# Side work moved in a one-core encoder block: two sums of squares, the state space set-up, and two last scalings

## The chip, the cores and the metric

The kernel runs on one core of one Trainium2 chip. The metric is the device time of one execution in microseconds (us), as the median of three runs. The core has a matrix engine (TensorE, PE in the profile, with its weight loads as PEld), a vector engine (VectorE, DVE), an engine for functions of one operand (ScalarE, ACT), a general engine (GpSimd, POOL), and a queue that issues most DMAs (SyncE, SP). Each engine runs its own instructions strictly in order and waits on semaphores for the others.

## The reference

One layer of an encoder block on 1024 tokens of 1024 channels, in float32. Cut to what matters:

```python
h = h + 0.5 * swiglu(rms_norm(h, ffn1_norm), w_gate1, w_up1, w_down1)   # 1024 -> 2816 -> 1024
u = rms_norm(h, mix_norm);  z = u @ w_in
q, k, v, s_in, gates = split(z)
y_attn = neighbourhood_attention(q, k, v, rpb) @ w_attn_out
y_ssm  = s5_branch(s_in, lam, log_dt, b, c, d, glu) @ w_ssm_out         # state space layer, both directions
h = h + (g_attn * y_attn + g_ssm * y_ssm) @ w_out
h = h + 0.5 * swiglu(rms_norm(h, ffn2_norm), w_gate2, w_up2, w_down2)
h = h + (p @ w_ple) * sigmoid(rms_norm(h, ple_norm) @ w_ple_gate)
return rms_norm(h, final_norm)
```

`rms_norm(x, g)` is x * rsqrt(mean(x*x) + eps) * g over the channels.

## The kernel before

The activations are kept transposed, channels on the 128 partitions and tokens along the row, as eight channel tiles times two token halves `h[j][t]` of 128x512. A float32 product is made of three faster products: each operand is split into a rounded part and a rest (`split`, L152 to L154: a cast on ACT, a subtraction on DVE that writes `xl`, `wl` or `al`), and `mm3` (L181 to L186) multiplies high by high, high by low and low by high. One `mm3` is called a product here; it takes three PE instructions.

The two feed-forward layers use Strassen's scheme in its form with seven products (`Seven`, `Ffn`). A first tile of hidden units is computed plainly in four groups ("C" items: `11`, `12`, `22`, `21`, named after token half and column half). Layer 1 makes these groups with plain float32 matmuls (L651, two passes each), layer 2 with `mm3`. Then come ten pairs of hidden tiles p = 1 to 10 ("A" items, seven steps i, a gate `g` and an up branch `u` each, 14 items of 4 products per pair), and then the down projection ("B" items). The accumulators of an A pair are PSUM banks named x, y, z (`gx`, `ux`, ...). The bank `gx` is used by step 1, read out on DVE (L575), added to by step 3, used anew by step 5, read out again by L575, and added to by step 6. PE can't start step 3 or 6 before DVE has read the bank.

PE's order is the order in which the program is written. Side work is written as Python generators and driven by `tick()`, which is called after every product (in the plain groups after every L651 matmul): `yield n` means go on n products later. One generator chain runs beside layer 1:

- `early` (L351) norms the input: it waits 10 products, sums the squares of token half 0 over the channels with a matmul against a constant matrix (`stat`, `ms<-acc,ones`), takes the root (`rstd`: ACT's L205, then three DVE steps L206 to L208), scales the tiles (L349), and does the same later for half 1.
- `sums` makes the operands of the seven products.
- `gen_all` (L980) sets up the state space layer: `gen_params` is some 90 small DVE operations on 128x32 vectors (`pvec`, `pw`, `g_prm`); then for each of 16 pairs of state groups `gen_pair` builds matrices on POOL (`gm`, `em`, `bd`; L899 to L933), and `fin` turns them on PE 25 products later (40 for the last two): four transposes `tp` (L941) and four small matmuls `kp` (L952). After them 4 more products pass before the next pair.

Beside layer 2 runs `s7.second(10, 1)` (L364 on), which does for token half 1 what `early` does: after 10 products `ms<-acc,ones` (L251), the root, and the normed and split tiles for the groups `22` and `21`.

During the first part (up to the start of p = 2) the orders of PE, DVE and ACT are as written. From there to the last stage only PE's is; DVE's, ACT's, POOL's and SP's follow a planner that simulates the program and fills in what it finds ready, with some evacuations of PSUM ahead of the rest (`tc.high_priority`). Moving an item in the program therefore moves others too. The last stage, `end()` (L1676 on), is again in written order on DVE and ACT: the last two channel tiles (6 and 7) of the last 256 tokens are finished, the squares are summed, the root is taken, and `finish` multiplies (L1671) and stores pairs of tiles.

Of the kernel before, what the change touches and what calls it, by code (L numbers as in the profile page):

```python
# [25 lines left out]
NPAIR = 16  # L26
# [12 lines left out]
def encoder_block(ctx, tc, I, out):  # L39
# [38 lines left out]
    def thid(name, shape=(P, HT), dt=F32R):  # L78
        return at("hid", shape, dt, name)
# [4 lines left out]
    def tmq(name, shape=(P, HT)):  # L84
        return at("tmp", shape, F32, name)

    def bank(name):
        return ps.tile([P, HT], F32, tag="ps", name=name)
# [37 lines left out]
    def start(gen):  # L126
        side["gen"], side["wait"] = gen, next(gen, None)
        if side["wait"] is None:
            side["gen"] = None
# [71 lines left out]

        return tc.issue_after(mark["ins"]) if "ins" in mark else nullcontext()

    def rstd(m, r, q):
        A.activation(r, m, AF.Abs_reciprocal_sqrt, bias=eps)  # L205
        V.tensor_tensor(q, r, r, ALU.mult)  # L206
        V.scalar_tensor_tensor(q, m, eps, q, ALU.add, ALU.mult)
        V.scalar_tensor_tensor(r, q, -3.0, r, ALU.add, ALU.mult)  # L208

    class Norm:  # L210
# [30 lines left out]
            T.matmul(self.acc, lhsT=ones, rhs=sq, start=self.rest is None, stop=last)  # L241
            self.rest = sq

        def stat(self, r=None, summed=False):
            if summed:
                m = self.acc
            else:
                m = bank("ms")[:, 0:self.n]
                sums = [self.acc] + self.more
                for i, sq in enumerate(sums):  # L250
                    T.matmul(m, lhsT=ones, rhs=sq, start=i == 0, stop=i == len(sums) - 1)  # L251
            q = tmq("rq", [P, self.n])
            r = thid("rs", [P, self.n], F32) if r is None else r
            rstd(m, r, q)
            self.r = r

        def apply(self, gi, res, every):
# [35 lines left out]
    def after(n, fn):  # L293
        def gen():
            yield n
            fn()
        return gen()

    def chain(*gens):
        for g in gens:  # L300
            yield from g
# [8 lines left out]
    class Seven:  # L310
# [39 lines left out]

        def early(self):  # L351

            yield 10
            self.stat(0)
            for j in range(NK):
                self.gain(j, 1)
            yield 2
            for j in range(NK):
                self.scale(j, 0)
            yield 6  # L360
            for j in range(NK):
                self.add(j, 1)
            yield 2
            for k in range(4):  # L364
                self.put("a12", self.h[4 + k][0])
                yield 1
            yield 5
            self.stat(1)
            for k in range(4):
                self.put("a11", self.h[k][0])  # L370
            yield 6
            for j in (0, 4, 1, 5, 2, 6, 3, 7):
                self.scale(j, 1)
            yield 1
# [507 lines left out]
    def load_bc(pr):  # L882
        if pr < NPAIR:
            bcs[pr] = pools["g"].tile([P, 6, 2, 16], F32, tag="bc", bufs=1, name="bc")
            nc.sync.dma_start(bcs[pr], I["ssm_bc"][pr])
# [92 lines left out]
    s7 = Seven(h, 0, up)  # L978

    def gen_all():  # L980
        while "g" not in pools:
            yield 1
        yield from gen_params()
        load_bc(0)
        yield 10
        for pr in range(NPAIR):
            fin = gen_pair(pr)
            yield 25 if pr < NPAIR - 2 else 40
            fin()
            yield 4  # L990

# [8 lines left out]
    ffn = Ffn(s7, I["wg1"], I["wu1"], I["wd1"], a1_d, load_x, done, t0_done, (4, 7))  # L1000
# [581 lines left out]
    for n_, (i, j) in enumerate(steps):  # L1582
        if n_ == 4:
            s7 = Seven(h, 2)
            ffn = Ffn(s7, I["wg2"], I["wu2"], I["wd2"], a2_d, load_h2, done, t0_done2, (8, 11))
# [28 lines left out]
        ple_w(1)  # L1614

    ffn.hooks["B", 6, 2] = ple_ahead
    start(chain(s7.second(10, 1), ffn.sums(2)))
    ffn.run()
    drain()

# [15 lines left out]
    fin = [Fin(i) for i in range(3)]  # L1636

    def products(m, part):
        t, c0, c1 = parts[part] if part < 3 else (1, 0, HT)
        n = c1 - c0  # L1640
        a, b = bank("pg")[:, 0:n], bank("pp")[:, 0:n]
        for k in range(NK):
            mm3(a, W[m][k], [x[:, c0:c1] for x in pn[t][k]], k == 0, k == NK - 1)
            tick()
        for k in range(2):
            mm3(b, wpp[m // 4][(m % 4) * 2 + k], [x[:, c0:c1] for x in phl[k, t]], k == 0, k == 1)
            tick()
        return a, b, tmp("ps", [P, n]), h[m][t][:, c0:c1]
# [5 lines left out]
    def scaled(m, hm):  # L1654
        A.activation(hm, hm, AF.Copy, scale=gains[:, 4, m:m + 1])
# [22 lines left out]
    def end():  # L1678

        start(after(9, fin[1].stat))  # L1680
        six = products(6, 2)
        drain()
        finish(1, (0,))
        A.activation(six[2], six[0], AF.Sigmoid)
        added(*six)
        a, b, s, hm = products(7, 2)
        A.activation(s, a, AF.Sigmoid)
        fin[2].square(6, A)
        finish(1, (2,))

        A.activation(dummy, eps, AF.Abs_reciprocal_sqrt)
        scaled(6, six[3])
        added(a, b, s, hm)
        fin[2].square(7, V)
        scaled(7, hm)
        finish(1, (4, 6))
        fin[2].stat()
        finish(2)

    steps = [(m, 0) for m in range(4)] + [(m, 3) for m in range(4)] + [(m, 0) for m in range(4, NK)]  # L1700
# [109 lines left out]
```

## Time and profile before

| | us |
|---|---|
| median of 3 runs (lowest to highest) | 2099.49 (2098.23 to 2099.73) |
| the profiled execution, its own time | 2096.29 |
| its span, first to last instruction | 2094.5 |
| PE busy in the span | 2074.5 (99%) |
| DVE, ACT, POOL busy | 1416.1, 999.6, 399.4 |

The span is what the trace shows; 1.8 us of the profiled execution lie around it. The granted clock of TensorE was 0.998 of full speed over the whole span. PE is the engine to watch: what it does not compute, it waits, and every wait has a row with its releaser. Idle time of the others costs nothing by itself. A timeline row gives start, duration, engine, line, operation, shapes and, in brackets, how long the engine was idle before it and who ended that. Instructions of one engine overlap a little, so the next start can lie before the sum of start and duration.

### The profile page before, as it was taken

The numbers are of one execution on the slowest core, as the hardware profiler recorded it, in microseconds if no ns is written. First come the engines' busy times: TensorE is split into PE (matmuls) and PEld (weight loads), VectorE is DVE, ScalarE is ACT, GpSimd is POOL, SyncE is SP. The second block draws the span as 40 slices with busy tenths as digits, with TensorE's granted clock in tenths as the row PEclk, the third lists the DMA queues.
The fourth block names the chain that finished last, engine by engine and source line by source line (L and its number), as shares of the span: only waits on it lengthen the run. The fifth ranks groups of instructions, "written<-read, shape, count | busy, mean of one in ns | idle before, by whom it ended". The sixth has DMA issues, their size and how long they took to land.

```text
span 2094.5 us, 28063 instructions
## 1 busy us (share of the span) xinstructions
PE 2074.5 (99%) x9662; PEld 1705.4 (81%) x9662; DVE 1416.1 (68%) x2420; ACT 999.6 (48%) x1832; POOL 399.4 (19%) x636
## 2 busy tenths in 40 slices
PE   8999999999999999999999999999999999999998
PEld 3788888888888888888898888788888888888886
DVE  7897776667967334677753668995665665786855
ACT  6434333334445333667774635643333334445543
POOL 0037556441000006888200001000000000000000
PEclk9999999999999999999999999999999999999999
DMA  3435444475533551233477745243324238433302
GB/s 134 143 118 154 125 135 120 144 270 169 188 114 111 159 189 64 70 97 98 123 208 260 247 145 117 77 150 121 100 86 135 82 121 297 155 106 94 118 21 81
DMA packets 197744, 285.19 MB, mean 136 GB/s; under 512 B 41569, under 2 KB 81121, under 8 KB 197601
## 3 DMA queue, kind: packets, MB, share of 16 engines
q1 hardware_dynamic: 180304, 258.20, 38.8%
q10 hardware_dynamic: 14992, 21.00, 3.0%
q0 software_dynamic: 2304, 4.20, 1.2%
q8 instruction: 76, 1.25, 0.2%
q14 instruction: 68, 0.55, 0.1%
HBM read 201.01 MB, written 82.31 MB: 135 GB/s over the span
## 4 chain that ended last, share of the span: by engine, by line
PE 94%; DVE 2%; ACT 1%; DMA 1%; SPq 0%; issue 0%; DVEq 0%; ACTq 0%
PE dx L184 4%; PE dx L185 4%; PE dx L186 4%; PE gx L184 3%; PE ux L184 3%; PE ux L186 3%; PE gx L186 3%; PE gx L185 3%; PE ux L185 3%; PE gt L184 3%; PE gt L185 3%; PE gt L186 3%; PE dy L186 2%; PE dy L184 2%; PE dy L185 2%; PE gy L184 2%
## 5 line engine op out<-in xcount | busy, mean ns | idle before, releaser
L153 ACT CAST wh<-hbuf 128x512 fp32r<-128x512 f32 x280 | 173.0, 622 | 392.3 <-PE gx L185 80.9
L154 DVE TENSOR_TENSOR wl<-hbuf,wh 128x512 fp32r<-128x512 f32 x280 | 209.2, 750 | 122.7 <-ACT wh L153 120.5
L153 ACT CAST wh<-wblk 128x512 fp32r<-128x512 f32 x190 | 118.0, 622 | 192.6 <-PE dx L185 83.2
L154 DVE TENSOR_TENSOR wl<-wblk,wh 128x512 fp32r<-128x512 f32 x190 | 130.6, 690 | 49.3 <-ACT wh L153 41.8
L184 PE MATMUL dx<-ah,wh 128*128 128x512 f32 x416 | 163.3, 393 | 0.3 <-DVE hbuf L688 0.3
L186 PE MATMUL dx<-ah,wl 128*128 128x512 f32 x416 | 161.9, 389 | 0.0
L185 PE MATMUL dx<-al,wh 128*128 128x512 f32 x416 | 161.8, 389 | 0.0
L1092 POOL TENSOR_TENSOR sc<-X,rho 128x128 f32<-128x128 f32 x128 | 77.9, 609 | 327.2 <-ACT X L1075 317.3
L154 DVE TENSOR_TENSOR al<-araw,ah 128x512 fp32r<-128x512 f32 x154 | 106.3, 694 | 50.1 <-PE dx L185 21.1
L184 PE MATMUL gx<-xh,wh 128*128 128x512 f32 x320 | 124.9, 390 | 1.2 <-DVE c L575 1.2
L184 PE MATMUL ux<-xh,wh 128*128 128x512 f32 x320 | 125.0, 390 | 0.0
L186 PE MATMUL ux<-xh,wl 128*128 128x512 f32 x320 | 124.5, 389 | 0.0
L185 PE MATMUL gx<-xl,wh 128*128 128x512 f32 x320 | 124.5, 389 | 0.0
L186 PE MATMUL gx<-xh,wl 128*128 128x512 f32 x320 | 124.5, 389 | 0.0
L185 PE MATMUL ux<-xl,wh 128*128 128x512 f32 x320 | 124.5, 389 | 0.0
L153 ACT CAST ah<-araw 128x512 fp32r<-128x512 f32 x154 | 94.9, 619 | 43.2 <-PE dx L185 12.6
L184 PE MATMUL gt<-xh,wh 128*128 128x512 f32 x256 | 102.7, 401 | 0.0
L186 PE MATMUL gt<-xh,wl 128*128 128x512 f32 x256 | 99.8, 390 | 0.0
L185 PE MATMUL gt<-xl,wh 128*128 128x512 f32 x256 | 99.8, 390 | 0.0
L422 DVE TENSOR_TENSOR hbuf<-hbuf 128x512 f32<-128x512 f32 x120 | 91.4, 762 | 2.1
L184 PEld LDWEIGHTS dx<-ah,wh 128*128 128x128 f32 x416 | 78.1, 188 | 17.8 <-issue 0.7
L185 PEld LDWEIGHTS dx<-al,wh 128*128 128x128 f32 x416 | 78.1, 188 | 16.9 <-issue 0.7
(381 smaller groups left out, 5590.2 us busy)
## 6 DMA issues: line engine op xcount, KB each, us to landing
araw<-a_d SPq DMA_DIRECT2D x154, 256.0 KB
a_d<-c SPq DMA_DIRECT2D x148, 256.0 KB
wblk<-in_wd SPq DMA_DIRECT2D x88, 256.0 KB
hbuf<-in_wg SPq DMA_DIRECT2D x40, 512.0 KB
hbuf<-in_wu SPq DMA_DIRECT2D x40, 512.0 KB
wst<-in_win SPq DMA_DIRECT2D x26, 512.0 KB
hbuf<-in_xT SPq DMA_DIRECT2D x32, 256.0 KB
h_d<-hbuf ACTq DMA_DIRECT2D x32, 256.0 KB
```

The source lines that it names most:

```text
L153: A.copy(hi, src)
L154: return eng.tensor_tensor(lo, src, hi.bitcast(F32), ALU.subtract)
L184: T.matmul(o, lhsT=wh, rhs=xh, start=first, stop=False, skip_group_check=more)
L185: T.matmul(o, lhsT=wh, rhs=xl, start=False, stop=False, skip_group_check=more)
L186: T.matmul(o, lhsT=wl, rhs=xh, start=False, stop=last, skip_group_check=more)
L422: V.tensor_tensor(b11, (b12, b22, None, None, b21)[i - 2], b11, ALU.subtract)
L1092: G.tensor_tensor(sc, both, rho4, ALU.mult)
```

## The change

Three pieces of side work are written at other places; no arithmetic is added or taken away.

- Both sums of squares that a feed-forward layer takes beside its first products come two products later: `early` waits 12 instead of 10, and `second` 12 instead of 10.
- `gen_all` waits 56 products before `gen_params`, and the turned matrices stand 22 instead of 25 products behind their set-up. The transposes of the first pair come 53 products later in PE's order, those of each next pair 3 less, and from the fourteenth pair on 14.
- `rstd` gets a hook `mid` behind the root on ACT. In `end()` the two last scalings (L1655, tiles 6 and 7 times the gain) are given to it, so that ACT does them behind the last root instead of ahead of it.

```diff
-    def rstd(m, r, q):
+    def rstd(m, r, q, mid=None):
         A.activation(r, m, AF.Abs_reciprocal_sqrt, bias=eps)
+        if mid is not None:
+            mid()
         V.tensor_tensor(q, r, r, ALU.mult)
...
-        def stat(self, r=None, summed=False):
+        def stat(self, r=None, summed=False, mid=None):
...
-            rstd(m, r, q)
+            rstd(m, r, q, mid)
...
         def early(self):
 
-            yield 10
+            yield 12
             self.stat(0)
...
     def gen_all():
         while "g" not in pools:
             yield 1
+
+        yield 56
         yield from gen_params()
...
             fin = gen_pair(pr)
-            yield 25 if pr < NPAIR - 2 else 40
+            yield 22 if pr < NPAIR - 2 else 40
...
-    start(chain(s7.second(10, 1), ffn.sums(2)))
+    start(chain(s7.second(12, 1), ffn.sums(2)))
...
         A.activation(dummy, eps, AF.Abs_reciprocal_sqrt)
-        scaled(6, six[3])
         added(a, b, s, hm)
         fin[2].square(7, V)
-        scaled(7, hm)
         finish(1, (4, 6))
-        fin[2].stat()
+        fin[2].stat(mid=lambda: (scaled(6, six[3]), scaled(7, hm)))
         finish(2)
```

The line numbers of the changed kernel are 2 higher from L207 on and 4 higher from L987 on.

PE at the start of layer 1, before, in its own order (`g` and `u` are the gate and up banks of group `11`, one plain product each; in brackets what an instruction waits for):

```order
L651 MATMUL g_183<-xg,wblk 128x512 [waits DMAHW1_49,Activation_49]
L651 MATMUL u_184<-xg,wblk 128x512 [waits DMAHW2_49]
L345 MATMUL ms<-acc_112,ones 128x512 [waits DVE_49]
L651 MATMUL g_183<-xg,wblk 128x512 [waits Activation_49]
L651 MATMUL u_184<-xg,wblk 128x512
```

and now, from the same two products on:

```order
L653 MATMUL g_183<-xg,wblk 128x512 [waits DMAHW1_49,Activation_49]
L653 MATMUL u_184<-xg,wblk 128x512 [waits DMAHW2_49]
L653 MATMUL g_183<-xg,wblk 128x512 [waits Activation_49]
L653 MATMUL u_184<-xg,wblk 128x512
L347 MATMUL ms<-acc_112,ones 128x512 [waits DVE_49]
```

The sum of squares of half 0 stands behind the twelfth product instead of the tenth. The second one (`ms<-acc_113`) moves by two products as well, and the DVE operations that depend on them keep their order but for five that trade places with neighbours before 61 us.

DVE at steps 4 and 5 of p = 1, before (`g_prm` are the loaded state space parameters, `c` the hidden tiles, `wl` the rests of weights, `pvec` the set-up's vectors, `hbuf` the weight blocks that Strassen's scheme subtracts from each other):

```order
L422 TENSOR_TENSOR hbuf<-hbuf 128x512
L753 TENSOR_SCALAR g_prm<-g_prm 128x32
L780 TENSOR_SCALAR g_prm<-g_prm 128x32
L154 TENSOR_TENSOR wl<-hbuf,wh 128x512
L575 TENSOR_TENSOR c_621<-gy,c_621 128x512
```

and ten rows further:

```order
L581 TENSOR_TENSOR c_581<-c_600,c_581 128x512
L154 TENSOR_TENSOR wl<-hbuf,wh 128x512
L754 TENSOR_SCALAR pvec<-g_prm 128x32
L154 TENSOR_TENSOR wl<-hbuf,wh 128x512
L755 TENSOR_SCALAR pvec<-pvec 128x32
L422 TENSOR_TENSOR hbuf<-hbuf 128x512
```

Now, at the same two spots:

```order
L424 TENSOR_TENSOR hbuf<-hbuf 128x512
L755 TENSOR_SCALAR g_prm<-g_prm 128x32
L782 TENSOR_SCALAR g_prm<-g_prm 128x32
L154 TENSOR_TENSOR wl<-hbuf,wh 128x512
L577 TENSOR_TENSOR c_621<-gy,c_621 128x512
```

```order
L583 TENSOR_TENSOR c_581<-c_600,c_581 128x512
L154 TENSOR_TENSOR wl<-hbuf,wh 128x512 x2
L424 TENSOR_TENSOR hbuf<-hbuf 128x512
L426 TENSOR_TENSOR hbuf<-hbuf 128x512
L583 TENSOR_TENSOR c_738<-ux,c_738 128x512
```

The two clamps of `g_prm` stay where they were, and so does the load of `g_prm` in SP's order; the rest of the set-up, from the old L754 on, leaves this stretch and stands one pair p later.

PE in the group `11` of layer 2 (`u` is its up bank; one row is one of a product's three instructions, - before, + now):

```order
-L251 MATMUL ms<-acc,ones 128x512
+L184 MATMUL u_13097<-xh,wh 128x512
+L185 MATMUL u_13097<-xl,wh 128x512
+L186 MATMUL u_13097<-xh,wl 128x512
+L184 MATMUL u_13097<-xh,wh 128x512
+L185 MATMUL u_13097<-xl,wh 128x512
+L186 MATMUL u_13097<-xh,wl 128x512
+L253 MATMUL ms<-acc,ones 128x512
```

The sum of squares of half 1 stands two products later here too. On ACT the last root now stands ahead of the two scalings `hbuf<-hbuf,gains 128x256`, which stood ahead of it.

## Rows read from the trace of the kernel before

**Rows 1.** The page's first part: each engine's busy us, share of the span, instructions.

```profile
PE 2074.5 (99%) x9662; PEld 1705.4 (81%) x9662; DVE 1416.1 (68%) x2420; ACT 999.6 (48%) x1832; POOL 399.4 (19%) x636
```

**Rows 2.** Who PE waited for (first and last of eleven): us, times, longest.

```profile
PE g L651 <- ACT xg L336: 5.0, 1, 5.0
...
PE v L1393 <- DVE wl L154: 0.2, 1, 0.2
```

**Rows 3.** Timeline of PE at the start: both sums of squares among the products.

```profile
14.69 1.02 PE L651 MATMUL u<-xg,wblk 128*128 128x512 f32 x2
16.53 1.12 PE L345 MATMUL ms<-acc,ones 128*128 128x512 f32 x2 [0.82 <-DVE acc L341]
17.49 1.02 PE L651 MATMUL g<-xg,wblk 128*128 128x512 f32 x2
...
33.80 1.02 PE L345 MATMUL ms<-acc,ones 128*128 128x512 f32 x2
```

**Rows 4.** Timeline of ACT and DVE in the same stretch: roots, and what follows them.

```profile
17.70 0.69 ACT L205 ACTIVATE rs<-ms,eps 128x512 f32<-128x512 f32 x1 [0.64 <-PE ms L345]
...
35.58 0.69 DVE L206 TENSOR_TENSOR q<-rs 128x512 f32<-128x512 f32 x1 [0.32 <-ACT rs L205]
...
60.78 2.50 DVE L154 TENSOR_TENSOR wl<-hbuf,wh 128x512 fp32r<-128x512 f32 x4 [1.20 <-ACT wh L153]
```

**Rows 5.** Timeline of DVE and PE at steps 4 to 6 of p = 1.

```profile
92.58 0.18 DVE L753 TENSOR_SCALAR g_prm<-g_prm 128x32 f32<-128x32 f32 x1 [0.58 <-DMA g_prm<-in_ssm_p]
...
97.92 0.68 DVE L575 TENSOR_TENSOR c<-gx,c 128x512 f32<-128x512 f32 x1
...
98.76 0.47 PE L184 MATMUL gx<-xh,wh 128*128 128x512 f32 x1 [1.21 <-DVE c L575]
```

**Rows 6.** Timeline of DVE and POOL while POOL builds matrices, and PE's first transposes.

```profile
154.64 1.88 POOL L920 TENSOR_TENSOR em<-em,tg 128x576 f32<-128x576 f32 x1
...
148.82 1.65 DVE L536 TENSOR_TENSOR c<-c,c 128x512 f32<-128x512 f32 x1
...
157.71 0.68 DVE L575 TENSOR_TENSOR c<-gx,c 128x512 f32<-128x512 f32 x1
...
158.68 0.39 PE L184 MATMUL gx<-xh,wh 128*128 128x512 f32 x1
...
160.07 0.60 PE L941 MATMUL tp<-ident,gm 128*128 128x128 f32 x4
```

**Rows 7.** Timeline of DVE and PE at step 5 of p = 3, and DVE at a later pair of matrices.

```profile
174.18 0.69 DVE L575 TENSOR_TENSOR c<-gx,c 128x512 f32<-128x512 f32 x1 [0.76 <-PE gx L186]
...
176.70 0.39 PE L184 MATMUL gx<-xh,wh 128*128 128x512 f32 x1
...
226.49 1.66 DVE L422 TENSOR_TENSOR hbuf<-hbuf 128x512 f32<-128x512 f32 x1
228.07 1.92 DVE L532 TENSOR_TENSOR c<-c,c 128x512 f32<-128x512 f32 x1
```

**Rows 8.** Timeline of PE and DVE at the start of layer 2.

```profile
1341.07 1.12 PE L251 MATMUL ms<-acc,ones 128*128 128x512 f32 x2 [0.77 <-DVE acc L224]
...
1342.26 0.40 PE L185 MATMUL u<-xl,wh 128*128 128x512 f32 x1
...
1358.92 0.69 DVE L154 TENSOR_TENSOR xl<-hbuf,xh 128x512 fp32r<-128x512 f32 x1
...
1362.03 0.39 PE L185 MATMUL g<-xl,wh 128*128 128x512 f32 x1
```

**Rows 9.** Timeline of PE, ACT and DVE in the last stage.

```profile
2084.60 0.70 PE L251 MATMUL ms<-sq,ones 128*128 128x256 f32 x2 [0.70 <-DVE sq L232]
...
2084.57 0.89 ACT L1655 ACTIVATE hbuf<-hbuf,gains 128x256 f32<-128x256 f32 x2
2085.37 0.45 ACT L205 ACTIVATE rs<-ms,eps 128x256 f32<-128x256 f32 x1
...
2087.29 2.50 DVE L1671 TENSOR_TENSOR hbuf<-hbuf,rs 128x512 f32<-128x512 f32 x4
```

## The prediction

> **What bounds the kernel now.** First the page's first part: PE is busy for 2074.5 of 2094.5 us [rows 1], so the change can only give back what PE waits, and what PE computes is the same on both sides. So the next view is the list of PE's waits: eleven, the longest 5.0 us for the first operand, the shortest 0.2 us [rows 2]. Then the timelines around those that the change touches: 0.82 us ahead of the first sum of squares [rows 3], 1.21 us at step 6 of p = 1 [rows 5], 0.77 us ahead of the sum in layer 2 and 0.70 us ahead of the last one [rows 8, 9]. Between 100 and 640 us, where the set-up of the state space layer runs, PE waits nowhere. That sets the scale: all four waits together are 3.5 us, and about 0.2% of the time, 4.2 us, is what a measurement of this kernel can tell from no change.
>
> **The first sum of squares, two products later.** A plain product takes PE 0.858 us: 19 of them lie between 17.49 and 33.80 [rows 3]. Two are 1.72 us, and the wait that they fill is only 0.82. In the new order the sum starts three products behind the one at 14.69, at 17.26 instead of 16.53. It takes 1.02 us within a stream and took 1.12 after the stall [rows 3], so it ends at 18.28 instead of 17.65, and the root on ACT, which waited for nothing else [rows 4], starts 0.63 us later. PE itself is ahead: the next product but two started at 17.49 + 1.72 = 19.21 and now starts at 18.12, a gain of 1.09 us.
>
> Who waits for the root? DVE, and all behind it: from 18.4 us on DVE works through without a gap until it waits 0.32 us for the second root [rows 4]. That root comes from the second sum, which stands two products later on a PE that is 1.09 us ahead, so it is 1.72 - 1.09 = 0.63 late as well. Nothing in between gives the time back. The new DVE order brings the scaling of group `22` one split forward, which would free ACT's weight casts earlier, but in ACT's order that split's cast now stands behind it; DVE then waits its 1.20 us [rows 4] one row earlier, and the first weight rest starts where it did. From 60.78 to 98 us DVE and ACT wait for each other in turn and for the load of `g_prm` (0.58 us), not for PE. At 98.76 PE waits for the last of this chain, the read-out of bank `gx` that starts at 97.92 [rows 5].
>
> So I take it that the chain arrives 0.63 us later and PE with it: the 1.09 us gained are waited away there and **0.63 us are lost**. The bounds: -1.09 if the chain has slack that I don't see, +0.63 if it has none. I take the upper end, because the rows show DVE or ACT at work, or one waiting for the other, all the way.
>
> **The set-up, 56 products later.** The stall at 98.76 looks like the set-up's: DVE waited 0.58 us at 92.58 for `g_prm` [rows 5]. But the two clamps that wait for this load, and the load itself, keep their places in DVE's and SP's orders; only what is behind them moves, by 56 products of 0.68 us (29 lie between 1342.26 and 1362.03 [rows 8]), 38 us. So this wait stays, and the relief comes where PE had no wait to lose: zero.
>
> Moving it could cost something. PE's transposes come 53 products, 36.1 us, later in PE's order, so set-up and POOL have 3 products, 2.0 us, less. POOL finished the first `em` at 154.64 + 1.88 = 156.5, and PE began the transposes at 160.07 [rows 6]: 3.5 us of cover, and the set-up's last step now stands two items (5.4 us) earlier within its pair p. Later pairs follow each other every 26 products instead of 29; 26 x 0.68 + 1.7 for PE's own work is 19.4 us, and the first pair, set-up copies included, took POOL 15.5. SP and ACT get the same loads, stores and copies in other places; the weights that stand behind them on SP are two pairs p ahead. Cost zero, covered by these margins; the bound above is the second rival.
>
> While POOL builds a matrix, DVE slows: a `c<-c` took 1.65 us at 148.82 and a `c<-c,c` 1.92 at 228.07, against 0.69 otherwise, but a read-out of a PSUM bank stayed at 0.68 [rows 6, 7]. The Trainium skill says why (SBUF — State Buffer, Who interferes with whom): a VectorE instruction with two SBUF inputs contends with a GpSimd instruction that reads SBUF, for a lock and not for a share, and one with a single SBUF input doesn't. The trace agrees, with 1.65 and 0.68 us. By that rule the same POOL work costs DVE the same wherever it stands, which adds nothing to the sum as long as DVE's lag is covered.
>
> **The sum in layer 2, two products later.** Here the products are short. The last instruction ahead of the sum ended at 1341.07 - 0.77 = 1340.30; instructions take 0.39 us [rows 7] and start every 0.68 / 3 = 0.227, so it began at 1339.91. Six more follow, then the sum at 1341.50, the next product at 1342.36 and its second instruction at 1342.58. Before, that instruction stood at 1342.26 + 1.36 = 1343.62 [rows 8]: **1.04 us gained**. The sum ends at 1341.50 + 1.02 = 1342.52 instead of 1342.19, so the root is 0.33 us late. The tightest reader is the eighth product of group `22`: its operand's rest was done at 1358.92 + 0.69 = 1359.61, and PE read it at 1362.03 [rows 8]. Now it is done 0.33 later, and 0.60 more for one read-out that stands ahead of it, at 1360.54, and PE comes at 1360.99. Cover 0.45 us: no new wait. Bounds: -1.04, and 0 if the late root is paid back in group `22`.
>
> **The last scalings.** The two scalings took 0.89 us on ACT and the root started at 2085.37, right behind them [rows 9]. But it also needs the last sum. At the start a root began 17.70 - 16.53 = 1.17 us behind its sum [rows 3, 4]; this sum has half the columns and took 0.42 less (0.70 against 1.12), so it could let the root start at 2084.60 + 0.75 = 2085.35. I take 0.02 us gained; the bounds are 0 and 0.42 (one pass of the sum, 0.35 us, as its end). Behind the root the scalings are done by 2086.7, and the multiplication that reads them is the fourth of those from 2087.29 on, at 2089.1 [rows 9]: covered by 2.4 us.
>
> **The sum.** 2096.29 + 0.63 + 0 - 1.04 - 0.02 = 2095.86 for the profiled execution, 0.43 below it. That execution was 3.2 us faster than the median of the runs, so against the median I say 2099.49 - 0.43 = **2099.1**.
>
> **The rivals.**
>
> *The front keeps its gain.* If DVE's chain isn't the bound up to 98 us, or the planned order shortens it, the 1.09 us stay: -1.09 - 1.04 - 0.02 = -2.15, 2097.3. For it: PE's wait at 98.76 is for a single read-out. Against: DVE's gapless rows from 18 us on.
>
> *POOL's work falls on the tight read-out: slower.* Step 6 follows step 5 on the same bank, and DVE's read-out has 176.70 - 174.18 - 0.69 = 1.83 us to spare [rows 7]. A matrix build costs DVE about an extra 1 us for each of two or three operations (1.66 and 1.92 against 0.69 [rows 7]). By PE's orders, before, the builds began 10, 8 and 6 products ahead of the end of step 5's gate item at the nearest, and now two begin 7 and 3 ahead of it, one just behind it, and one just behind the up branch's item, four products later. If 3 us of lag meet 1.83 us of margin, each such pair costs some 1.2 us plus 0.2 for the restart. Up to four pairs lie so: +1.4 to +5.6, with the rest of the sum 2100.5 to 2104.7, and with two pairs 2101.9. It decides from 1.83 us of lag on. For it: the first build in the old order put DVE so far behind that a read-out which started at 157.71 left 0.3 us to the product at 158.68 [rows 6]. Against: in all later pairs PE never waited. By the Trainium skill's rule above this is where the contention would show.
>
> *The move takes the `g_prm` wait away after all.* If the load lands earlier, 0.58 + 0.18 us leave the chain: 2098.3.
>
> **How the numbers follow.** The forecast 0.60, the front keeping its gain 0.13, POOL's work on the read-out 0.21, `g_prm` 0.06. The range takes in the first rival, the second with two pairs, and the scatter of the runs (1.3 us below the median at the lowest): 2096.2 to 2102.3. Only the far end of the second rival is slower by over 4.2 us, and no case is faster by as much: faster 0.02, same 0.94, slower 0.04.
>
> **What would show it.** In the changed kernel's trace: no wait ahead of either moved sum; the first root at about 18.33; the wait at step 6 of p = 1 grown from 1.21 to more than 2 us and ending at about 99.4; DVE still waiting for `g_prm`; no PE wait at transposes; the next layer's sum without a wait; the last root at 2085.3 on the old clock. I am wrong if the wait at step 6 ends before 98.76, if PE waits between 100 and 500 us, or if the last root moves by over 0.4 us.

## The result, and the profile after

The changed kernel takes **2102.39 us** (median of 22 runs, 2099.17 to 2104.97), the kernel before, in runs on the same chips, 2098.69 (22 runs, 2096.22 to 2101.46). The ratio is 1.0017 [1.0011, 1.0024]: slower by 3.7 us, where the forecast was no change that can be told, 2099.1, with a range up to 2102.3.

The profiled execution of the changed kernel took 2104.40 us, its span 2102.6, against 2096.29 and 2094.5. The page's first part, as [rows 1]:

```profile
PE 2078.0 (99%) x9662; PEld 1707.6 (81%) x9662; DVE 1419.2 (67%) x2420; ACT 999.6 (48%) x1832; POOL 396.9 (19%) x636
```

PE has the same 9662 instructions and is busy 3.5 us more; the rest of the 8.1 us of span is waiting. PE's waits, which answer to [rows 2] (us in total, times, longest us):

```profile
PE g L653 <- ACT xg L338: 4.9, 1, 4.9
PE gx L184 <- DVE c L577: 4.5, 3, 2.0
PE yo L1121 <- DVE ot L1246: 2.0, 1, 2.0
PE ux L184 <- DVE c L577: 1.0, 2, 0.8
...
PE v L1397 <- DVE wl L154: 0.6, 1, 0.6
```

The waits for `acc` are gone from it, both in the front and in layer 2, as meant. But the list has waits on the read-outs of `gx` and `ux` (DVE's `c`, line 577) that before had one entry of 1.2 us. The timeline of PE, at the two moved sums and the last one and at the waits (start, us, operation, in brackets the idle time and who ended it):

```profile
17.13 1.02 PE L347 MATMUL ms<-acc,ones 128*128 128x512 f32 x2
...
83.49 0.47 PE L184 MATMUL ux<-xh,wh 128*128 128x512 f32 x1 [0.79 <-DVE c L577]
...
99.22 0.47 PE L184 MATMUL gx<-xh,wh 128*128 128x512 f32 x1 [1.85 <-DVE c L577]
...
302.83 0.50 PE L184 MATMUL ux<-xh,wh 128*128 128x512 f32 x1 [0.22 <-DVE c L577]
...
468.03 0.50 PE L184 MATMUL gx<-xh,wh 128*128 128x512 f32 x1 [1.96 <-DVE c L577]
...
1045.72 0.49 PE L1121 MATMUL yo<-emi 128*128 128x128 f32 x2 [2.02 <-DVE ot L1246]
...
1349.56 1.02 PE L253 MATMUL ms<-acc,ones 128*128 128x512 f32 x2
...
1403.04 0.50 PE L184 MATMUL gx<-xh,wh 128*128 128x512 f32 x1 [0.74 <-DVE c L577]
...
2092.69 0.70 PE L253 MATMUL ms<-sq,ones 128*128 128x256 f32 x2 [0.71 <-DVE sq L234]
```

To see what each wait is worth, the start of each product after is set against the same product before. How far PE is behind, profile against profile, worked out from the starts of the same instructions on both sides:

| place | PE behind, us | added here |
|---|---|---|
| start | 0.0 | |
| behind step 6 of p = 1 (100 us) | 0.5 | 0.5 |
| behind the wait at 303 us | 1.1 | 0.55 |
| last pair p, step 5 to 6 (468 us) | 4.9 | 3.9 |
| 767 us (`v<-wl`, a load) | 5.4 | 0.5 |
| 1046 us (`yo`) | 8.1 | 2.7 |
| layer 2, the sum | 7.0 | -1.07 |
| layer 2, step 6 of p = 1 | 8.1 | 1.05 |

The rows at 767 and 1046 us aren't the change's: the wait at 767 us is 0.65 us here and 0.21 in the second profile of the same kernel, and the one at 1046 us is shown below with the kernel before alone. Without the front (0.5 us) and the wait at 1046 us (2.7), 4.9 us are left, and 3.9 of them are one place at 468 us.

### The profile page after: what moved, and what is told of

Its sections match the earlier page's. It is cut to its first block, busy times and chain, and to the rows that moved or that the text cites. A ratio compares the mean times of both kernels' runs of the same rounds, so it can differ in the third digit from the quotient of the medians.

```text
span 2102.6 us, 28061 instructions
## 1 busy us (share of the span) xinstructions
PE 2078.0 (99%) x9662; PEld 1707.6 (81%) x9662; DVE 1419.2 (67%) x2420; ACT 999.6 (48%) x1832; POOL 396.9 (19%) x636
## 4 chain that ended last, share of the span: by engine, by line
PE 89%; DVE 7%; DMA 2%; ACT 1%; issue 1%; SPq 0%; DVEq 0%; ACTq 0%
PE dx L184 4%; PE dx L185 4%; PE dx L186 4%; PE gx L184 3%; PE ux L184 3%; PE gx L186 3%; PE gx L185 3%; PE ux L185 3%; PE ux L186 3%; PE gt L184 3%; PE gt L186 3%; PE gt L185 3%; PE dy L185 2%; PE dy L186 2%; PE dy L184 2%; PE gy L184 2%
## 5 line engine op out<-in xcount | busy, mean ns | idle before, releaser
L186 PE MATMUL dx<-ah,wl 128*128 128x512 f32 x416 | 161.9, 389 | 0.0
```

Of the source, the lines that this page charges most:

```text
L186: T.matmul(o, lhsT=wl, rhs=xh, start=False, stop=last, skip_group_check=more)
```

## The experiments

**Which part costs it.** Only the set-up's two numbers are put into the kernel before:

```diff
 # e1_setup_only: kernel before, with
+        yield 56
-            yield 25 if pr < NPAIR - 2 else 40
+            yield 22 if pr < NPAIR - 2 else 40
```

> Only the state space set-up is moved (56 products later, matrices 22 apart); sums of squares and last scalings stand as before. Theory A (the moved matrices run into the first loads of the down projection, SP holds those loads back, DVE waits for one of them ahead of the read-out of gx, PE stalls about 2 us near 468 us and then runs some 3 us at the lower clock): about 2102 us, with that wait in the trace, and the wait at step 6 of p = 1 at its old 1.2 us. Theory B (the late roots cost the time): no different from before, 2098.7 us, no wait of over 0.5 us between 100 and 700 us.

Measured 2101.64, ratio 1.0016 [1.0007, 1.0025]. Its profile has the wait near 468 us, at 1.24 us and without a lower clock behind it, and the old 1.20 us at step 6 of p = 1. The other way round, the changed kernel with the set-up put back:

```diff
 # e2_no_setup: kernel after, with
-        yield 56
-            yield 22 if pr < NPAIR - 2 else 40
+            yield 25 if pr < NPAIR - 2 else 40
```

> The two later sums and the scalings behind the last root, the set-up as before. Theory A: 2098.5 us, within 1 us of before (0.5 us lost at step 6 of p = 1, where the wait is about 1.8 us, and up to 1.0 us gained in layer 2), no wait between 100 and 700 us. Theory B: about 2102 us.

Measured 2098.75, 1.0001 [0.9992, 1.0010]. So the set-up has the loss, and the three other edits together come out at nothing that these runs can tell. Both kernels unchanged once more, for the scatter between two profiles of one kernel:

> The kernel before once more, for a second trace. If the waits near 468 and 1046 us of the changed kernel come from the change, this trace has none over 0.5 us between 100 and 700 us and 0.7 us at the attention's first wait (1039 us); if they are scatter of the transfers, one of them may show here too.

> The changed kernel once more, for a second trace. Theory A: the wait for the read-out of gx near 468 us is there again, 1.5 to 2.5 us, and 0.2 us or more at 303 us. Scatter: it is not. The wait of 2.0 us at 1046 us hangs on a store of y, and may be anything from 0.7 to 2.

They took 2099.25 and 2101.34, one run each. In the kernel before, taken again, PE and DVE show at 1040 us (its line 1242 is 1246 after):

```profile
1040.40 0.49 PE L1117 MATMUL yo<-emi 128*128 128x128 f32 x2 [1.94 <-DVE ot L1242]
...
1036.32 0.56 DVE L1186 TENSOR_TENSOR row<-bt,rowm 128x384 f32<-128x384 f32 x1 [2.55 <-DMA y_d<-ys]
```

The wait ahead of `yo` was 0.66 us in the first profile of before and 1.94 in this one; after had 2.02 and then 0.74. It goes back to a store and is scatter, 2.7 of the 8.1 us. The wait at 468 us is not: none in both profiles of before, 1.96 and 2.31 in both of after. By the starts of the same products PE loses 3.9, 2.6 and 1.5 us at that place in after, after again and e1, and 0.5 to 0.6 at 303 us in each.

**Start or spacing.** Each number by itself, or nearly:

```diff
 # e6_spacing_only: kernel before, with
-            yield 25 if pr < NPAIR - 2 else 40
+            yield 22 if pr < NPAIR - 2 else 40
 # e7_spacing_18: kernel after, with
-            yield 22 if pr < NPAIR - 2 else 40
+            yield 18 if pr < NPAIR - 2 else 40
 # e15_start_50, e16_start_46: kernel after, with
-        yield 56
+        yield 50    (e16: yield 46)
```

> The kernel before with matrices 22 products apart, and no other part of the change: the set-up starts where it did, the last pair is turned some 42 products (29 us) earlier than before. Theory A (the late end of the matrices is what costs): no wait for gx or ux between 440 and 500 us, 2098.7 us. Theory C (the shorter spacing brings POOL's work onto the tight read-outs, wherever it stands): one to three waits of 0.2 to 1.2 us between 150 and 450 us, each with some 0.3 us to get going, 2099.5 to 2102 us.

> The changed kernel with matrices 18 instead of 22 products apart: the set-up starts 56 products later as in the change, but the fourteenth pair is turned some 42 products earlier than before. Theory A: no wait for gx near 468 us, 2099.5 us or less. If POOL can't follow (22 products and 1.7 us of PE's own make 16.7 us a pair, against 15.5 us that the first pair took POOL), PE waits at transposes, by up to 1 us a pair, and the time is over 2102 us.

> The changed kernel with the set-up 50 instead of 56 products later: every pair of matrices stands 4 us earlier, and the stretch from 440 to 470 us still has one pair's stores and loads beside the down projection's loads, as in the changed kernel. On SP the stores of the pair that is built near 435 us now stand some three rows further ahead of the first load for the down projection. Theory A6 (in the changed kernel SP stands for POOL and for DVE at that pair's load and stores, and the first load for the down projection comes at 441.3 instead of 434.0 us; the operand that DVE waits for follows 20 to 22 us behind it): the first of these loads at 437 to 438 us, the operand's load at 457 to 459 us, PE's wait for gx or ux near 468 us under 0.6 us, and 2099.8 us. Theory A2 (the traffic of the pairs beside these loads): the wait stays at 1.2 to 2.3 us, and 2102 us.

> The changed kernel with the set-up 46 instead of 56 products later (7 us earlier than in the changed kernel, and the last pairs 4 products later than in the kernel before). Theory A6: the first load for the down projection at 434 to 436 us, no wait of PE near 468 us or one under 0.3 us, 2099.2 us. If anything that ends later than before is costly: still over 2101 us.

Spacing 22 with the old start: 2098.70, 0.9999 [0.9990, 1.0008]. Spacing 18 with the new start: 2100.27, 1.0006 [0.9997, 1.0015]. Neither can be told from before, and neither has a wait for `gx` near 468 us, though both have short ones for `ux` there (0.37 and 0.25 us) and one or two of about 0.2 us earlier. The first theory had said none of these, and for spacing 18 at most 2099.5 us. So no run shows that the later start costs by itself, where the last pairs of matrices still come early.

Starts of 50 and 46: 2103.17, 1.0021 [1.0012, 1.0030], and 2102.22, 1.0017 [1.0008, 1.0025], where the theory that it is SP's late loads (A6) had said 2099.8 and 2099.2. Both forecasts fell. The wait for `gx` did shrink, to 0.54 and 0.59 us, but `ux` has 1.30 and 0.26 close behind it, and there are other waits between 180 and 262 us. Set against before by the starts of the same products, e15 loses 2.4 us at those earlier places and 2.5 near 470 us, e16 1.0 and 1.5. So in these profiles two things cost: where the last pairs fall, and where POOL's work falls. Starts of 50 and 46 had less wait for `gx` by the first and lost more by the second. The next views take them in turn.

**The wait at 468 us.** There DVE reads bank `gx` out for PE between step 5 and step 6 of the last pair p, and an operand of the down projection that follows (`araw`, its cast `ah`, its rest `al`) stands ahead of the read-out in DVE's order. A row of `SPq` or `ACTq` is the issue of a DMA. `a_d` takes the gated hidden tiles that the down projection reads back as `araw`, `e_d` and `f_d` take the finished matrices of a pair, and `bc` is what the next pair is built from. The changed kernel's timeline of SP, ACT, DVE and POOL:

```profile
433.18 0.33 SPq L887 DMA_DIRECT2D bc<-in_ssm_bc  x1
...
441.27 4.07 SPq L603 DMA_DIRECT2D wblk<-in_wd  x5
...
451.01 2.00 SPq L603 DMA_DIRECT2D wblk<-in_wd  x3
...
461.89 0.58 SPq L604 DMA_DIRECT2D araw<-a_d  x1
...
457.87 0.33 ACTq L949 DMA_DIRECT2D f_d<-fm  x1
458.31 0.25 ACT L958 COPY ka<-kp 32x128 f32<-32x128 f32 x1 [8.41 <-DMA wblk<-in_wd]
...
465.65 0.62 ACT L153 CAST ah<-araw 128x512 fp32r<-128x512 f32 x1 [2.92 <-DMA araw<-a_d]
...
466.31 1.06 DVE L154 TENSOR_TENSOR al<-araw,ah 128x512 fp32r<-128x512 f32 x1 [2.25 <-ACT ah L153]
467.29 0.68 DVE L577 TENSOR_TENSOR c<-gx,c 128x512 f32<-128x512 f32 x1
...
465.65 1.17 POOL L921 TENSOR_TENSOR tg<-g_pe,bc 128x576 f32<-128x576 f32 x1
```

And of the kernel before:

```profile
433.96 0.38 SPq L601 DMA_DIRECT2D wblk<-in_wd  x1
...
455.52 0.40 SPq L602 DMA_DIRECT2D araw<-a_d  x1
...
461.44 0.62 ACT L153 CAST ah<-araw 128x512 fp32r<-128x512 f32 x1 [1.37 <-DMA araw<-a_d]
...
462.70 0.68 DVE L575 TENSOR_TENSOR c<-gx,c 128x512 f32<-128x512 f32 x1
```

Read them from SP on. Before, the first load of the down projection's weights stands between two stores `a_d`, and a matrix pair's stores `e_d` come a dozen loads later. After, a pair's load `bc` and its four stores `e_d` fall ahead of that first load, and SP issues in order. SP's waits in this stretch (430 to 475 us) name POOL, which still reads the old `bc`:

```profile
SPq L887 <- POOL bd L933: 6.3, 1, 6.3
```

Counted from PE's start of step 5, the first weight load goes from 25.5 us ahead to 19.2 ahead, the first `araw` load from 3.9 ahead to 1.4 behind, its cast from 2.0 to 5.2, DVE's read-out from 3.3 to 6.8. A read-out that starts up to 4.9 us behind step 5 costs PE nothing: the 1.6 us of margin are gone and 1.96 us of wait are there. Of the 3.5 us that the read-out is later, the cast brings 3.2. The other 0.4 is POOL's: the rest `al` took 1.06 us beside POOL's `tg<-g_pe,bc`, and 0.69 before and in e5, where POOL had no work beside it.

What the rows don't name, the instructions of the traces do. Between 430 and 475 us each DMA that SP or ACT issues stands behind a wait for one of eight semaphores, which the program takes in turn over both engines. So a DMA goes out only when the eighth ahead of it has landed (all 59 of them in before, all 60 in after). The first `araw` load went out at 461.89, 0.06 us after its eighth had landed. ACT had filled `fm` at 449.9; the eighth ahead of its store `f_d` was SP's load of `wblk` at 452.68 (the last of the three from 451.01 on), which landed at 457.79. Now the late `araw` can be added up. The weight loads start 6.3 us later. Between the first of them and `araw` lie 29 DMAs instead of 34, which at the 0.63 us each of before is 3.2 us less. But each now takes 0.71 us, 2.2 us more over the 29. Together that is 5.3 us, which is what `araw` is late.

Three things were named for it: POOL's build of matrices slowing DVE, SP's stand for POOL, and ACT's 8.4 us of idleness. These runs part them, each from the changed kernel (e13 from the kernel before):

```diff
 # e5_bc_on_pool: the pair's load off SP
-            nc.sync.dma_start(bcs[pr], I["ssm_bc"][pr])
+            nc.gpsimd.dma_start(bcs[pr], I["ssm_bc"][pr])
 # e9_ka_free: a buffer of its own for ka
-        ka = pools["g"].tile([32, 240], F32, tag="ka", bufs=1, name="ka")
+        ka = tmp("ka")[0:32, 0:240]
 # e12_fd_on_pool, e13_before_fd_on_pool: ACT's store on POOL's queue
-        nc.scalar.dma_start(f_d[pr], fm)
+        nc.gpsimd.dma_start(f_d[pr], fm)
 # e14_fd_bc_on_pool: both DMAs on POOL's queue
 # e17_pair12_later: the late pair turned behind SP's first loads
+            if pr == 12:
+                yield 12
```

> The changed kernel with one edit: the small load of bc for the next pair of state groups is issued from POOL's own queue and no longer from SP, which in the changed kernel stood 6.3 us at 433 us for POOL, with the loads of the down projection behind it. The orders of PE, DVE and ACT are those of the changed kernel. Theory A1 (SP is held up there, so the loads come late): no wait, or one under 0.5 us, for the read-out of gx near 468 us, and about 2099.5 us. Theory A2 (the matrices' own stores and loads fill the DMA engines beside the down projection's loads): the wait stays at 1.2 to 2.3 us, and 2102 us. In both the 0.2 us at 303 us stay.

> The changed kernel with one edit: ka, the small block of lag products that ACT and DVE fill for each pair of state groups and that SP stores, is taken from the rotating work tiles and no longer from its one buffer, so that its next filling need not wait for the last store. Up to 470 us the orders of PE, DVE and ACT are those of the changed kernel. Theory A3 (the store of ka lies 20 us behind the weights of the down projection, ACT and DVE stand 8 to 9 us for its buffer, and all that is behind them comes late): no idle time of over 3 us ahead of the filling of ka near 450 us, the read-out of gx near 468 us in time (no wait of PE, or under 0.4 us), and 2099.0 us. Theory A2 (the transfers alone are late): the wait for gx stays at 1.2 to 2.3 us, and 2101.5 us. The 0.2 us at 303 us stay in both.

> The changed kernel with one edit: the store of the turned matrices (fm) is issued from POOL's queue and no longer from ACT's. In the changed kernel ACT had filled fm at 449.9 us and issued this store at 457.87, 8 us later, with the filling of ka and all weight casts behind it; what it waited for was the end of an earlier transfer on SP's side. Theory A4 (ACT stands at its own store, since the down projection's loads fill the queues): ACT's and DVE's idle time ahead of ka near 450 us falls from 8.4 and 9.4 to under 3 us, PE's wait for gx near 468 us to under 0.4 us, and the time to 2099.5 us. Theory A2 (the down projection's operands are late by themselves, as the DMA engines are full): the idle time goes, but PE's wait stays at 1.2 to 2.3 us, and 2101.5 us.

> The kernel before with the same edit, as a control: there ACT stood 2 us at this store near 440 us, and PE waited nowhere between 100 and 700 us. No difference, 2098.7 us, no wait of PE there, if the edit itself costs and gives nothing; over 2100 us if issuing from POOL has a price of its own, which would then be part of the run above.

> The changed kernel with both the store of fm and the load of bc issued from POOL, so that neither ACT nor SP stands for them. If both hold-ups together make the wait at 468 us: no wait there, 2099.2 us, with 0.5 us left at 303 us. If the operands are late by themselves: 1 us or more of wait is left, over 2100.5 us.

> The changed kernel with one edit: the thirteenth pair of matrices (and so the three behind it) starts 12 products later, so that its load and stores stand on SP behind the first loads for the down projection, as in the kernel before, and no longer ahead of them. The first twelve pairs and all else are those of the changed kernel; the last pairs end still later than in it. Theory A6 (SP is held by that pair's load and stores, which wait for POOL, with the down projection's loads behind them): counted from PE's step 5 of p = 10, the first of these loads 25.5 us ahead instead of 19.2, the first operand's load 3 to 4 us ahead instead of 1.4 behind, no wait of PE near 468 us (under 0.4 us), the wait of 0.2 us at 303 us kept, and 2099.7 us. Theory A2 (late matrices cost by their traffic or their end): the wait stays at 1.2 us or more, and 2102 us or over.

What the runs gave at this place, in us from PE's start of step 5, beside their medians less that of before, run with them:

| kernel | first weight load | first `araw` load | cast `ah` | read-out of `gx` | PE's wait `gx` (`ux`) | time less before |
|---|---|---|---|---|---|---|
| before | -25.5 | -3.9 | 2.0 | 3.3 | 0 | 0 |
| e9 | -19.8 | 0.0 | 3.8 | 5.4 | 0.50 | 1.9 |
| e15 | -23.9 | -0.3 | 4.1 | 5.4 | 0.54 (1.30) | 4.2 |
| e16 | -23.4 | -1.5 | 4.2 | 5.5 | 0.59 (0.26) | 3.2 |
| e13 | -24.6 | -2.2 | 4.2 | 5.5 | 0.60 (0.29) | 2.3 |
| e1 | -19.2 | 0.7 | 4.5 | 6.1 | 1.24 | 3.0 |
| e5 | -19.2 | 1.0 | 5.1 | 6.4 | 1.51 | 1.7 |
| after | -19.2 | 1.4 | 5.2 | 6.8 | 1.96 | 3.7 |
| e14 | -21.8 | 3.0 | 7.3 | 8.6 | 3.70 | 6.7 |
| e12 | -21.4 | 3.5 | 7.9 | 9.2 | 4.31 | 9.2 |
| e17 | -27.2 | -4.9 | 6.4 | 9.5 | 4.60 | 6.8 |

(e6, e7 and e8 have the first weight load 25.5 us ahead and the read-out at 4.7 to 4.9, and no wait for `gx`.) Wherever there is a wait for `gx`, it is the read-out's start less 4.9 us, and but for e17 the later `araw` is loaded, the later its cast, give or take a microsecond. That is the near cause of this wait, and all these profiles show it; the last column shows that the time holds more than this wait. Then one by one:

*e5*, 2100.60, 1.0009 [1.0000, 1.0018]: the first weight load did not come earlier by a tenth, though `bc` had left SP. SP's longest wait in the stretch was now

```profile
SPq L528 <- DVE c L532: 8.2, 1, 8.2
```

a store `a_d` of the gated product, for DVE. So SP's wait for POOL was not what held the loads; it lay beside this one. What holds them is what SP still issues behind the next `a_d`: the pair's four stores and three more `a_d`. From that `a_d` to the first weight load it is 5.8 us in e5 as in after, and 0.4 before.

*e9*, 2100.37, 1.0009 [1.0000, 1.0018]: ACT still stood 6.9 us ahead of `ka`, so `ka`'s buffer (A3) does not hold ACT. The median lies 1.8 us nearer to before than that of after, though the two intervals overlap. POOL's order had shifted with the edit, and the waits at 303 and 468 us were 0 and 0.50 instead of 0.22 and 1.96.

*e12*, 2107.61, 1.0048 [1.0035, 1.0061]: ACT's hold-up is gone, and all is worse:

```profile
452.81 0.25 ACT L958 COPY ka<-kp 32x128 f32<-32x128 f32 x1 [0.34 <-PE kp L954]
...
470.89 0.62 ACT L153 CAST ah<-araw 128x512 fp32r<-128x512 f32 x1 [7.22 <-DMA araw<-a_d]
...
472.94 0.79 PE L184 MATMUL gx<-xh,wh 128*128 128x512 f32 x1 [4.31 <-DVE c L577]
```

The copy `ka` waits 0.34 us instead of 8.41, but `araw` comes later still: 34 DMAs lie again between the first weight load and it, at 0.73 us each. That ACT's hold-up alone is the cause (A4) fell. Its control e13, the same edit before, 2100.69, 1.0013 [1.0004, 1.0022], puts 2.3 us on the edit itself. With `bc` off SP as well, e14 had 2105.04, 1.0035 [1.0022, 1.0047], and 3.70 us of wait, so taking both hold-ups away doesn't bring the operand in time either.

*e17*, 2106.43, 1.0034 [1.0022, 1.0046]: SP's loads are as early as before, and still PE waits 4.60 us, for now ACT stands:

```profile
459.75 0.26 ACT L958 COPY ka<-kp 32x128 f32<-32x128 f32 x1 [0.22 <-PE kp L954]
...
467.70 0.33 ACTq L949 DMA_DIRECT2D f_d<-fm  x1
468.07 0.24 ACT L959 COPY ka<-kp 32x112 f32<-32x112 f32 x1 [8.06 <-DMA wblk<-in_wd]
...
468.35 0.16 DVE L960 TENSOR_TENSOR ka<-ka,kp 32x16 f32<-32x16 f32 x1 [9.41 <-ACT ka L959]
...
472.02 0.56 PE L184 MATMUL gx<-xh,wh 128*128 128x512 f32 x1 [4.60 <-DVE c L577]
```

The store `f_d<-fm` stands in ACT's order ahead of the second copy of `ka`. It went out only when an earlier load of `wblk` had landed (its eighth, issued by SP at 462.27 and landed at 467.63); behind it stood ACT's copy and the cast of `ah`, and behind those DVE and PE. So the forecast for this run fell too, but it showed the second hold-up alone: a pair of matrices that is turned in the middle of the burst of weight loads stops ACT for 8 us at its own store, and one that is turned ahead of it puts its stores ahead of the loads on SP. Either way the first operand is late. In e17 the store ended last. In after the load did: ACT had caught up by then and stood idle for 2.92 us ahead of the cast.

What stays open: why each DMA takes longer there. There is more traffic (316 GB/s from 450 to 500 us against 276 before), but no run changed the traffic alone. Nor did any run with a later start and pairs 22 apart both lose this wait and win the time back.

**303 us: POOL's work on a read-out.** This is the second rival, small in the changed kernel. Its DVE and POOL:

```profile
299.64 1.81 DVE L424 TENSOR_TENSOR hbuf<-hbuf 128x512 f32<-128x512 f32 x1
...
302.09 0.68 DVE L577 TENSOR_TENSOR c<-ux,c 128x512 f32<-128x512 f32 x1
...
299.02 1.88 POOL L922 TENSOR_TENSOR em<-em,tg 128x576 f32<-128x576 f32 x1
```

and e9, where PE and DVE have the same order and POOL is at copies:

```profile
300.20 0.69 DVE L424 TENSOR_TENSOR hbuf<-hbuf 128x512 f32<-128x512 f32 x1
...
301.54 0.68 DVE L577 TENSOR_TENSOR c<-ux,c 128x512 f32<-128x512 f32 x1
...
299.56 0.70 POOL L934 COPY bd<-bb 64x64 f32<-64x64 f32 x1
```

DVE's addition takes 1.81 us beside POOL's product of two SBUF operands and 0.69 beside its copies of 64x64; the read-out is 0.55 us later and PE waits 0.22, with 0.55 in all there. The Trainium skill's rule (SBUF — State Buffer, Who interferes with whom), which the prediction weighed, agrees with the 1.81 us, and with the read-outs, of one SBUF operand each, at 0.68. In e15 the same work costs more, here at the second of its three early waits:

```profile
219.27 1.96 POOL L922 TENSOR_TENSOR em<-em,tg 128x576 f32<-128x576 f32 x1
...
219.97 1.81 DVE L426 TENSOR_TENSOR hbuf<-hbuf 128x512 f32<-128x512 f32 x1
...
222.44 0.50 PE L184 MATMUL ux<-xh,wh 128*128 128x512 f32 x1 [0.79 <-DVE c L577]
```

**The front and `g_prm`.**

```diff
 # e11_early_11: kernel before, with
-            yield 10
+            yield 11
 # e8_clamps_later: kernel before; the clamps write elsewhere, so that DVE may place them later
-        V.tensor_scalar(x, x, -87.3, 88.0, ALU.max, ALU.min)
+        V.tensor_scalar(q, x, -87.3, 88.0, ALU.max, ALU.min)
...
-        V.tensor_scalar(lr, lr, -1.0e-4, None, ALU.min)
+        lr, raw = c32("lrc"), lr
+        V.tensor_scalar(lr, raw, -1.0e-4, None, ALU.min)
```

> The kernel before with the first sum of squares one product later instead of two. One product is 0.86 us, against a wait of 0.82 or 0.61 us. If PE's time up to 99 us is set by the chain from the first root alone: no wait ahead of the first sum, the wait at step 6 of p = 1 grown from 1.2 to about 2.0 us, and PE at that step neither earlier nor later than before, counted from its first product (within 0.3 us). If PE's lead is kept: the wait at step 6 stays near 1.2 us, and PE is 0.8 us earlier there.

> The kernel before with the two clamps of g_prm written into the set-up's own vectors, by which they stand some twelve DVE rows later, and DVE need not wait for that load at 92.6 us. If DVE's chain from the first root to the read-out at step 6 of p = 1 is what PE waits for, PE's wait there falls from 1.2 to about 0.4 us (0.58 of wait and 0.18 of a clamp leave the chain), and 2098.0 us. If something else ends last there, it stays at 1.2 us.

With the sum one product later (2098.40, one run), PE:

```profile
16.84 1.12 PE L345 MATMUL ms<-acc,ones 128*128 128x512 f32 x2 [0.30 <-DVE acc L341]
...
99.06 0.47 PE L184 MATMUL gx<-xh,wh 128*128 128x512 f32 x1 [1.85 <-DVE c L575]
```

0.5 us of wait less at the sum [rows 3], 0.6 more at step 6 [rows 5]: what PE gains ahead of the root it waits away there. Without the clamps' wait (2100.36, 1.0009 [1.0000, 1.0018]), PE there:

```profile
98.89 0.47 PE L184 MATMUL gx<-xh,wh 128*128 128x512 f32 x1 [1.20 <-DVE c L575]
```

Still 1.20 us: the 0.58 us for `g_prm` lay beside DVE's wait for ACT's cast, which is 0.74 us once the clamps are gone. That kernel lost time elsewhere, for one a wait of 1.09 us at 161.9 us for POOL's `em`, 5 us later.

**Layer 2 alone.**

```diff
 # e10_second_only: kernel before, with the last scalings' edit and
-    start(chain(s7.second(10, 1), ffn.sums(2)))
+    start(chain(s7.second(12, 1), ffn.sums(2)))
```

> The kernel before with two parts of the change: the later sum of squares of layer 2, and the scalings behind the last root. The first sum and the set-up stand as before. If the parts add up as the traces so far say: PE's wait at step 6 of p = 1 in layer 1 at its old 1.2 us, no wait ahead of the sum in layer 2, 1.0 us gained there and 0.5 given back at step 6 of p = 1 in layer 2, so 0.5 us less than before, 2098.3 us. If the gain in layer 2 is lost altogether: 2098.8.

2099.10, 1.0000 [0.9991, 1.0009], too coarse to part 2098.3 from 2098.8. In the profile PE gains 1.07 us at the sum and loses 0.45 again at step 6 of p = 1; in after the loss was 1.05. On the way DVE waits for a load:

```profile
1382.43 0.69 DVE L424 TENSOR_TENSOR hbuf<-hbuf 128x512 f32<-128x512 f32 x1 [1.92 <-DMA hbuf<-in_wu]
```

All 12 profiles with the sum two products later have this wait (1.15 to 2.26 us), and one of the 7 with it in the old place (1.00). The loss follows it: in all 12 it is this wait less 0.9 us, from 0.28 us with a wait of 1.15 to 1.38 with 2.26. Why the load comes later, and whether the loss goes when the wait is taken away, was not tried.

## Why the prediction was wrong, step by step

- **The set-up, "Cost zero, covered by these margins": wrong, and this step alone makes the miss.** It measured 3.0 us (e1). The sentence that failed is that "the weights that stand behind them on SP are two pairs p ahead". It holds in the middle of the stretch, not at its end: near 440 us the loads of the down projection start, and the read-out behind their first operand has 1.6 us of margin. The step looked at the pairs of matrices by PE's, DVE's and POOL's orders. For SP and ACT, in whose orders the stores moved, it had one margin for all pairs.
- **The second rival** named the bank and the engine (DVE's read-out between steps 5 and 6, 2101.9 with two pairs) and had 0.21. Its mechanism, POOL's work, is there, but in the changed kernel it gave 0.55 us at 303 us, on `ux`, and 0.4 of the wait on `gx` at 468 us; the rest of that wait came by the late load on SP. That its time was close is luck. With other starts it costs more (2.4 us in e15).
- **The front, 0.63 lost: right, as far as the clock stays.** In the profile 0.5; the root started at 18.19 (18.33 said), the next step-6 wait ended at 99.22 (99.4 said). The wait there is 1.85 and not over 2, because 0.79 of it fell at 83.5, at the bank `ux`, which I had not seen. The first rival, a kept gain, fell. But in four of the eleven profiles with this sum two products later (e12, e14, e16, e17) the granted clock fell behind this wait, and PE lost 1.6 us more (2.1 in e16, whose wait was 2.40); the sum had no term for that.
- **`g_prm`: right** that its wait costs PE nothing, and e8 shows why.
- **Layer 2: the gain right (1.04 said, 1.07), the rest missed.** I looked for the tightest reader in group `22` alone; the 0.45 to 1.05 us were paid back at step 6 of the next pair p, where the read-out had 1.5 us to spare before.
- **The last scalings: 0.02 said, 0.03 found at the root.** It starts 0.74 us behind its sum's start (0.77 before), and the scalings stand behind it as said. That is too small to tell from the times:

```profile
2093.43 0.47 ACT L205 ACTIVATE rs<-ms,eps 128x256 f32<-128x256 f32 x1 [0.68 <-PE ms L253]
2093.80 0.90 ACT L1659 ACTIVATE hbuf<-hbuf,gains 128x256 f32<-128x256 f32 x2
```

- **The chances: 0.94 for no change that can be told**, with 4.2 us as the least that can. That limit was too wide: 22 runs of each kernel tell 3.7 us, with an interval of 2.3 to 5.0. And every slower case was priced by POOL alone. That PE waited nowhere there tells that the old order's margins held; a step that is moved by 38 us meets others.

## What to carry to other kernels

When a step is moved, follow each of its DMAs on its queue to the end of the step's whole run, and look there for the first transfers of the next stage: those have little lead, and a store in front of them may cost PE. Where DMAs of two engines take their semaphores in turn, a store of the one can also wait for a load of the other. A read-out that stands behind an operand of the next stage in DVE's order makes PE wait for that operand's load. And a wait that is taken away ahead of a chain comes back where PE next reads the chain's result.

## What the runs showed of the hardware

- A DMA that ACT issues can stop ACT's compute: its store stood 8 us (8.41 in after, 8.06 in e17) until a load that SP had issued was done. The trace shows it as a wait for a semaphore that the program shares between the DMAs of both engines. The Trainium skill (DMA: Bandwidth & Descriptors, Issuing engines are not separate DMA queues) says that DMAs started by several engines run on the same 16 engines; no run here shows what that sharing alone costs.
- The same wait may cost its length or twice that. Behind the wait of 1.96 us the granted clock fell to about half (the 1.2 GHz level) for some 3 us, and behind one of 2.31 us in the other profile of the same kernel it didn't. Windows of after, and one of e4 (from:to, us, then each engine's busy us and instructions, granted clock, DMA share, GB/s):

```profile
470.00:473.00 3.00, 3.00 (x9) 2.29 (x8) 1.94 (x4) 0.92 (x2) 0.00 (x0) 0.53 0.95 324
473.00:480.00 7.00, 7.00 (x32) 5.77 (x31) 4.88 (x9) 2.57 (x5) 0.00 (x0) 1.00 1.05 396
```

```profile
471.00:474.00 3.00, 3.00 (x15) 2.49 (x14) 2.85 (x5) 1.77 (x4) 0.00 (x0) 1.00 0.98 320
```

Nine instructions in 3 us against 15: about 1.6 of the 3.9 us that the profile lost there. It is the same at step 6 of p = 1 in layer 1: behind waits of 1.84 to 1.88 us the granted clock stayed in eight profiles and fell in three (e12: 0.69 from 99 to 102 us, 0.74 from 102 to 105). What decides it stayed open.
